# VectorE makes all weight remainders in both feed-forward products, with three edits at the borders between the stages

## The chip, the cores and the metric

One NeuronCore of a Trainium2 chip runs the whole program. The metric is the device time of one execution in microseconds (us). The kernel before was run three times: 2825.05, 2814.47 and 2814.90 us, median 2814.9 us.

## What is computed

Two layers of a decoder trunk, for 1024 prompt tokens and 32 sample tokens that share all weights. Layer 0 has a pooling and attention mixer, layer 1 a gated mixer; each is followed by a feed-forward block and a gated embedding. The change touches the feed-forward blocks only:

```python
D_MODEL = 1024; D_FF = 4 * D_MODEL
...
r = r + y                                   # after the mixer
h = rmsnorm(r, norm_ffn[i])
r = r + jnp.einsum('nlf,fd->nld', jnp.square(jax.nn.relu(jnp.einsum('nld,df->nlf', h, ffn_w1[i]))), ffn_w2[i])
h = rmsnorm(r, norm_ple[i])
gate = jax.nn.sigmoid(jnp.einsum('nld,de->nle', h, ple_w_gate[i]))
r = r + gate * jnp.einsum('nlp,pd->nld', p[i], ple_w_proj[i])
```

## The kernel before

**Tiles.** Activations lie with features on the 128 partitions and all 1056 tokens along the row. Every float32 operand is split in two: a rounded part that TensorE takes (`whi` for weights, `sh` for activations) and the remainder (`wlo`, `sl`). A product is the sum of three matmuls, whi·sh, whi·sl and wlo·sh. For weights, `w_split` (lines 147 to 165) has ScalarE copy the raw tile to `whi` (L153), and then another engine subtract it to give `wlo` (L157). That is GpSimd unless an engine is named; with `later=True` the subtraction is handed back as a function, for the caller to place. The subtraction also gives the raw tile's buffer back and starts the load of the next weights. `whi` and `wlo` have two buffers each, so the copy for the step after next starts when TensorE has finished the present step.

**Two products with seven multiplications.** `pair` runs the block of a layer ("0" and "1"; a third call, "m", does a mixer product and is left as it was). The first product makes the hidden activations in 8 chunks `c` of four tiles. Chunk 0 is plain (`gemm_phase`, evicted by `plain`); chunks 1 to 7 go through `product1`, seven multiplications `p` in the order 2, 4, 6, 1, 5, 3, 7, each on sums or differences of blocks. The second product runs `product2` for four `n`, seven `p` (order 4, 6, 2, 1, 5, 3, 7) and two halves `kt`. One multiplication of `product1` and one half of `product2` are both 48 matmuls of 264 columns. I call both a **unit**. `w_operand` makes the block sums of the weights on VectorE (L206, L210, L216, L217).

**What sets the order.** Engines' queues are written out by this program and worked off in the order written. `fill` is a clock that steps after every six matmuls, so eight steps make a unit; `fill.after(n, f)` writes f's instructions n steps later.

**Evictions.** In `product1`, `evac1` empties the PSUM bank of each of two `m`: ScalarE copies (L1301) for p = 4, 6, 2, VectorE adds (L1305) and scales (L1541) for the others. Multiplications that accumulate into a bank must wait for its eviction: 6 follows 4, and 5, 3, 7 follow 1. In `product2`, VectorE adds each of four banks to the residual tile `r` (L1494) after the second half, in the order m = 0, 3, 1, 2.

**Between the products.** `parts_of` takes a chunk's four hidden tiles, subtracts blocks (L1560, L1567; the functions t4 and minus) and stores the operands to DRAM, `hop` (L1551, L1561). The second product loads them back (`op_load`, L1409, into one `hx` and one `tmp` buffer) and splits them (`op_split`: ScalarE L1152, VectorE L1155). The pools `tmp` and `hx` have four buffers each; each chunk of `product1` takes two of either. `ahead2` does the first loads and splits while chunk 7 is multiplied. In the last `n`, `ple_piece` prepares the operands of the embedding block's product (ScalarE L257, L1603; VectorE L260; the sum of squares L1604 on GpSimd).

So a layer has three **borders**: (1) from the plain chunk 0 into chunk 1, (2) from the first product into the second, (3) from the second product into the embedding block (matmuls of L303).

## Time and profile before

| what | value |
|---|---|
| timed runs | 2814.47 to 2825.05 us, median 2814.9 |
| profiled execution | 2809.02 us, span of its instructions 2807.2 us |
| TensorE matmuls | 2663.4 us busy, 95% of the span |
| VectorE, ScalarE, GpSimd | 1753.1, 1119.9 and 1005.4 us busy |
| mean granted TensorE clock | 0.978 of full |

TensorE's busy share says that the sum of its pauses is small; where they are and what ended each is in the views quoted below. In those, PE is TensorE's matmuls, PEld its weight loads, DVE VectorE, ACT ScalarE, POOL GpSimd and SPq SyncE's DMA queue. Layer 0's feed-forward runs from 847 to 1489 us of the span, layer 1's from 2013 to 2659 us.

### The profile page before, as it was taken

The page shows a single profiled execution, that of the slowest core. Times are in us where ns is not written, and L with a number is a line of the kernel's source. Part 1 is how long each engine was busy: PE and PEld are TensorE (multiplying, and loading weights), DVE is VectorE, ACT ScalarE, POOL GpSimd, SP SyncE. Part 2 cuts the span into 40 slices and gives each one's busy share as a digit, 9 for nine tenths or more (in the row PEclk, how much of TensorE's full clock was granted, in tenths as well). Part 3 has the DMA queues.
Part 4 walks back from the last instruction along what each step waited for, and adds up shares of the span by engine and source line. Part 5 has one row for each costly group of instructions (what it writes and reads, how often), then busy time and mean ns, then how long its engine had stood idle before and what let it go on. Part 6 is the DMA issues. An engine that isn't in the chain of part 4 may idle for free. (4 is left out here: it accounts for less than half of the span.)

```text
span 2807.2 us, 48902 instructions
## 1 busy us (share of the span) xinstructions
PE 2663.4 (95%) x20190; PEld 2576.6 (92%) x20190; DVE 1753.1 (62%) x2370; ACT 1119.9 (40%) x1901; POOL 1005.4 (36%) x442
## 2 busy tenths in 40 slices
PE   8999999998988999999999999988899999999897
PEld 8998898987987999999999998988899999999896
DVE  7435435354375556788786455778745658887855
ACT  4343333334163333333344355234533343333543
POOL 3332233222253444222233343656344442222434
PEclk9999999999999999999999999999999999999998
DMA  5225334354634444744412223351344457343112
GB/s 170 73 86 134 97 113 138 104 143 153 221 127 156 145 145 146 276 170 154 146 55 78 89 80 96 73 168 47 133 124 157 146 180 281 133 141 127 51 64 102
DMA packets 159295, 366.53 MB, mean 131 GB/s; under 512 B 46528, under 2 KB 54752, under 8 KB 159072
## 3 DMA queue, kind: packets, MB, share of 16 engines
q1 hardware_dynamic: 158208, 362.59, 39.7%
q8 instruction: 159, 2.61, 0.4%
q10 hardware_dynamic: 864, 0.82, 0.1%
q14 instruction: 64, 0.52, 0.1%
HBM read 245.20 MB, written 105.15 MB: 125 GB/s over the span
## 5 line engine op out<-in xcount | busy, mean ns | idle before, releaser
L157 POOL TENSOR_TENSOR wlo<-wraw,whi 128x1024 fp32r<-128x1024 f32 x155 | 394.2, 2544 | 952.5 <-ACT whi L153 901.4
L157 POOL TENSOR_TENSOR wlo<-wr,whi 128x1024 fp32r<-128x1024 f32 x121 | 313.0, 2586 | 564.8 <-ACT whi L153 544.1
L1323 PE MATMUL PS<-sh,whi 128*128 128x264 f32 x2016 | 414.7, 287 | 36.0 <-ACT tmp L1301 21.3
L1479 PE MATMUL PS<-sh,whi 128*128 128x264 f32 x2016 | 408.0, 284 | 22.7 <-DVE r L1494 18.1
L1323 PE MATMUL PS<-sh,wlo 128*128 128x264 f32 x2016 | 414.6, 287 | 6.4 <-POOL wlo L157 6.2
L1323 PE MATMUL PS<-sl,whi 128*128 128x264 f32 x2016 | 414.2, 287 | 0.0
L1479 PE MATMUL PS<-sl,whi 128*128 128x264 f32 x2016 | 410.6, 286 | 1.2 <-DVE sl L1155 1.2
L1479 PE MATMUL PS<-sh,wlo 128*128 128x264 f32 x2016 | 410.4, 285 | 0.0
L1323 PEld LDWEIGHTS PS<-sh,whi 128*128 128x128 f32 x2016 | 318.8, 191 | 39.9 <-ACT tmp L1301 21.7
L153 ACT ACTIVATE whi<-wraw 128x1024 fp32r<-128x1024 f32 x181 | 191.5, 1058 | 370.8 <-DVE wraw L216 92.1
L1479 PEld LDWEIGHTS PS<-sh,whi 128*128 128x128 f32 x2016 | 314.1, 189 | 24.8 <-issue 20.2
L1323 PEld LDWEIGHTS PS<-sh,wlo 128*128 128x128 f32 x2016 | 316.3, 191 | 8.3 <-POOL wlo L157 8.3
L153 ACT ACTIVATE whi<-wr 128x1024 fp32r<-128x1024 f32 x153 | 162.3, 1061 | 394.5 <-PE PS L1479 267.5
L1323 PEld LDWEIGHTS PS<-sl,whi 128*128 128x128 f32 x2016 | 315.8, 190 | 0.0
L421 PE MATMUL g<-sh,whi 128*128 128x352 f32 x888 | 311.0, 350 | 4.1 <-DVE vsn L532 3.0
L1479 PEld LDWEIGHTS PS<-sl,whi 128*128 128x128 f32 x2016 | 312.9, 189 | 1.8 <-DVE sl L1155 1.8
L1479 PEld LDWEIGHTS PS<-sh,wlo 128*128 128x128 f32 x2016 | 313.8, 190 | 0.0
L423 PE MATMUL g<-sh,wlo 128*128 128x352 f32 x888 | 287.9, 324 | 0.0
L422 PE MATMUL g<-sl,whi 128*128 128x352 f32 x888 | 287.5, 324 | 0.0
L1494 DVE TENSOR_TENSOR r<-r,PS 128x528 f32<-128x528 f32 x252 | 168.2, 699 | 48.9 <-PE PS L1479 48.9
L421 PEld LDWEIGHTS g<-sh,whi 128*128 128x128 f32 x888 | 168.6, 190 | 25.9 <-issue 22.0
L1155 DVE TENSOR_TENSOR sl<-tmp,sh 128x528 fp32r<-128x528 f32 x124 | 168.0, 1388 | 25.4 <-ACT sh L1152 25.4
(340 smaller groups left out, 4697.6 us busy)
## 6 DMA issues: line engine op xcount, KB each, us to landing
hx<-hop SPq DMA_DIRECT2D x56, 528.0 KB, 4.6
tmp<-hop SPq DMA_DIRECT2D x56, 528.0 KB, 5.0
wr<-in_w SPq DMA_DIRECT2D x56, 512.0 KB, 4.3
hop<-tmp SPq DMA_DIRECT2D x108, 264.0 KB, 4.9
hop<-hx SPq DMA_DIRECT2D x84, 264.0 KB, 4.6
wr<-in_w1q SPq DMA_DIRECT2D x42, 512.0 KB, 4.1
wraw<-in_w_e SPq DMA_DIRECT2D x39, 512.0 KB, 3.3
rscr<-r SPq DMA_DIRECT2D x24, 528.0 KB, 3.0
```

The costliest lines, as they stand in the source:

```text
L153: ACT.activation(hi, raw, AF.Copy)
L157: (eng or POOL).tensor_tensor(lo, raw, hi.bitcast(F32), op=ALU.subtract)
L421: PE.matmul(ps[:, :CH], hi[:, ws], xh[:, cs], start=k == 0, stop=False)
L422: PE.matmul(ps[:, :CH], hi[:, ws], xl[:, cs], start=False, stop=False)
L423: PE.matmul(ps[:, :CH], lo[:, ws], xh[:, cs], start=False, stop=k == 7)
L1155: DVE.tensor_tensor(lo, x, hi.bitcast(F32), op=ALU.subtract)
L1323: PE.matmul(ps[:, n, :], a[:, ws], b[:, n * HT // 2:(n + 1) * HT // 2], start=first and k == 0 and i == 0, stop=k == 3 and i == 2, skip_gr ...
L1479: PE.matmul(ps[:, q, :], a[:, ws], b[:, q * HT // 2:(q + 1) * HT // 2], start=first and kt == 0 and k == 0 and i == 0, stop=kt == 1 and k ...
L1494: DVE.tensor_tensor(r, r, ps, op=ALU.add)
```

## The change

In layers 0 and 1: (a) `product1` no longer has GpSimd make the remainder; VectorE does, two steps behind the copy. (b) `product2` splits the weights at the third bank of both halves, the remainder on VectorE two steps later (before, one half did so, and the other had GpSimd make it). (c) The plain chunk's tiles 2 and 3 go to `hx` instead of `tmp`, and its block differences are written at steps 3, 6, 15, 22 like every other chunk's. (d) `ahead2` spreads eight operand splits over steps 34 to 48. (e) `ple_piece` adds its squares on VectorE.

```diff
@@ product1
-                    w_split(wptr[0] + 1)
+                    if l == "m":
+                        w_split(wptr[0] + 1)
+                    else:
+                        rest = w_split(wptr[0] + 1, DVE, True)
+                        if rest:
+                            fill.after(2, rest)
@@ ahead2
-                op_splits(0, k, 40 + k)
-                op_splits(2, k, 46 + k)
-            fill.after(47, lambda: op_load(1))
-            fill.after(53, lambda: op_load(3))
+                op_splits(0, k, 34 + 2 * k)
+                op_splits(2, k, 42 + 2 * k)
+            fill.after(46, lambda: op_load(1))
+            fill.after(54, lambda: op_load(3))
@@ product2
-                elif kt == 1 and i_m == 1 and not (last and p == 7):
-                    w_split(wptr[0] + 1)
-                elif kt == 0 and i_m == 2:
+                elif i_m == 2 and not (last and p == 7 and kt == 1):
                     rest = w_split(wptr[0] + 1, DVE, True)
                     if rest:
                         fill.after(2, rest)
@@ product2
-                    ple_piece(*pieces[p, kt, i_m], POOL, xp, gi)
+                    ple_piece(*pieces[p, kt, i_m], POOL if l == "m" else DVE, xp, gi)
@@ plain
-            u = h[0, j] = tmp()
+            u = h[0, j] = tmp() if j < 2 else h["pool"].tile([128, NT], F32, tag="hx", bufs=4, name=nm("hx"))
@@ begin
-            parts_of(c - 1, (1, 2, 4, 7) if c == 1 else (3, 6, 15, 22))
+            parts_of(c - 1, (3, 6, 15, 22))
```

VectorE's queue at border 1 of layer 0, from the first block difference of chunk 0 on. Before (`tmp_7745`, `tmp_7811`, `tmp_7920`, `tmp_8005` are the chunk's four tiles):

```order
L1567 TENSOR_TENSOR tmp_7745<-tmp_7745,tmp_7920 128x528
L1567 TENSOR_TENSOR tmp_7811<-tmp_7811,tmp_8005 128x528
L1567 TENSOR_TENSOR tmp_7745<-tmp_7745 128x528
L1567 TENSOR_TENSOR tmp_7811<-tmp_7811 128x528
L1567 TENSOR_TENSOR tmp_7920<-tmp_7920,tmp_7745 128x528
L1567 TENSOR_TENSOR tmp_8005<-tmp_8005,tmp_7811 128x528
L216 TENSOR_TENSOR wraw_7898<-wraw_7827,wr_7897 128x1024
L217 TENSOR_TENSOR wr_7894<-wr_7894,wr_7896 128x1024
```

The same place after the change (line 1567 has become 1570; `hx_7920` and `hx_8005` are tiles 2 and 3):

```order
L1570 TENSOR_TENSOR tmp_7745<-tmp_7745,hx_7920 128x528
L1570 TENSOR_TENSOR tmp_7811<-tmp_7811,hx_8005 128x528
L216 TENSOR_TENSOR wraw_7898<-wraw_7827,wr_7897 128x1024
L217 TENSOR_TENSOR wr_7894<-wr_7894,wr_7896 128x1024
L157 TENSOR_TENSOR wlo_8087<-wraw_7898,whi_8088 128x1024
L1570 TENSOR_TENSOR tmp_7745<-tmp_7745 128x528
L1570 TENSOR_TENSOR tmp_7811<-tmp_7811 128x528
L157 TENSOR_TENSOR wlo_8148<-wr_7896,whi_8149 128x1024
L1570 TENSOR_TENSOR hx_7920<-hx_7920,tmp_7745 128x528
```

The block sum of the weights, L216, now stands before the last four differences, and remainders (L157) stand between them.

VectorE's queue inside the second product of layer 0, one multiplication's four evictions and the next half. Before:

```order
L1494 TENSOR_TENSOR r_10963<-r_10963,PS 128x528
L1494 TENSOR_TENSOR r_10966<-r_10966,PS 128x528
L1494 TENSOR_TENSOR r_10964<-r_10964,PS 128x528
L1494 TENSOR_TENSOR r_10965<-r_10965,PS 128x528
L1155 TENSOR_TENSOR sl_97<-tmp_11278,sh_96 128x528 x2
L1155 TENSOR_TENSOR sl_83<-hx_11426,sh_82 128x528 x2
L157 TENSOR_TENSOR wlo_11614<-wr_8020,whi_11615 128x1024
```

The same place after the change (L1494 has become L1497):

```order
L1497 TENSOR_TENSOR r_10966<-r_10966,PS 128x528
L1497 TENSOR_TENSOR r_10969<-r_10969,PS 128x528
L1497 TENSOR_TENSOR r_10967<-r_10967,PS 128x528
L157 TENSOR_TENSOR wlo_11551<-wr_10979,whi_11552 128x1024
L1497 TENSOR_TENSOR r_10968<-r_10968,PS 128x528
L1155 TENSOR_TENSOR sl_97<-tmp_11278,sh_96 128x528 x2
L1155 TENSOR_TENSOR sl_83<-hx_11421,sh_82 128x528 x2
L157 TENSOR_TENSOR wlo_11614<-wr_8020,whi_11615 128x1024
```

A remainder has come in front of the fourth eviction.

VectorE's queue at border 3 of layer 0 (last `n`, where the second half of p = 3 is evicted), after the change (L1607 is the sum of squares that GpSimd made before):

```order
L157 TENSOR_TENSOR wlo_14306<-wr_10980,whi_14307 128x1024
L260 SCALAR_TENSOR_TENSOR sl_83<-r_10967,gains,sh_82 128x528
L1607 TENSOR_TENSOR acc<-acc,tmp_14332 128x528
L1497 TENSOR_TENSOR r_10970<-r_10970,PS 128x528
L260 SCALAR_TENSOR_TENSOR sl_85<-r_10968,gains,sh_84 128x528
L1607 TENSOR_TENSOR acc<-acc,tmp_14350 128x528
L1497 TENSOR_TENSOR r_10973<-r_10973,PS 128x528
L260 SCALAR_TENSOR_TENSOR sl_85<-r_10968,gains,sh_84 128x528
L1607 TENSOR_TENSOR acc<-acc,tmp_14368 128x528
L1497 TENSOR_TENSOR r_10971<-r_10971,PS 128x528
```

Before, the same rows stood there without the three L1607.

## Rows read from the trace of the kernel before

**Rows 1.** Who TensorE waited for, 820 to 1480: total, times, longest (us).

```profile
PE PS L1323 <- ACT tmp L1301: 10.7, 1, 10.7
PE PS L1479 <- DVE r L1494: 4.5, 1, 4.5
PE PS L1323 <- DVE tmp L1305: 3.1, 2, 2.5
```

**Rows 2.** Stretches inside the products: length, busy (count) per engine, clock, DMA share.

```profile
950.00:1000.00 50.00, 50.00 (x413) 50.00 (x412) 30.95 (x33) 19.68 (x26) 23.55 (x9) 1.00 0.43 149
1250.00:1300.00 50.00, 50.00 (x417) 50.00 (x417) 38.58 (x41) 18.87 (x28) 11.88 (x5) 1.00 0.49 161
```

**Rows 3.** The six borders in the same view, two rows a border, layer 0 first.

```profile
861.30:880.20 18.90, 8.13 (x52) 7.61 (x51) 5.10 (x6) 4.24 (x7) 4.73 (x2) 0.73 0.80 282
2026.40:2046.20 19.80, 9.07 (x50) 8.55 (x50) 5.10 (x6) 4.19 (x6) 4.73 (x2) 0.66 0.78 262
1142.90:1157.40 14.50, 9.53 (x64) 8.91 (x63) 13.55 (x16) 6.25 (x10) 3.12 (x2) 0.88 0.95 333
2309.90:2324.40 14.50, 9.72 (x64) 9.11 (x62) 13.61 (x16) 6.28 (x10) 3.13 (x2) 0.88 0.96 346
1468.50:1489.20 20.70, 13.75 (x98) 13.14 (x96) 18.91 (x17) 9.34 (x15) 14.95 (x8) 0.92 0.13 42
2636.90:2658.60 21.70, 14.79 (x98) 14.40 (x96) 18.79 (x17) 9.39 (x15) 14.82 (x8) 0.84 0.12 39
```

**Rows 4.** VectorE's groups by shape, 1200 to 1460: busy us, mean ns, idle before.

```profile
L1155 DVE TENSOR_TENSOR sl<-tmp,sh 128x528 fp32r<-128x528 f32 x45 | 67.1, 1527 | 12.0 <-ACT sh L1152 12.0
L1494 DVE TENSOR_TENSOR r<-r,PS 128x528 f32<-128x528 f32 x91 | 60.9, 699 | 18.9 <-PE PS L1479 18.9
L1155 DVE TENSOR_TENSOR sl<-hx,sh 128x528 fp32r<-128x528 f32 x44 | 28.9, 697 | 0.0
L157 DVE TENSOR_TENSOR wlo<-wraw,whi 128x1024 fp32r<-128x1024 f32 x9 | 11.0, 1223 | 3.2 <-ACT whi L153 2.9
```

**Rows 5.** VectorE in order of time at border 1: start, us, instruction, idle before.

```profile
858.97 1.32 DVE L1567 TENSOR_TENSOR tmp<-tmp,tmp 128x528 f32<-128x528 f32 x2
864.60 1.41 DVE L1567 TENSOR_TENSOR tmp<-tmp 128x528 f32<-128x528 f32 x2 [4.31 <-DMA hop<-tmp]
867.39 1.42 DVE L1567 TENSOR_TENSOR tmp<-tmp,tmp 128x528 f32<-128x528 f32 x2 [1.38 <-DMA hop<-tmp]
868.73 1.22 DVE L216 TENSOR_TENSOR wraw<-wraw,wr 128x1024 f32<-128x1024 f32 x1
```

**Rows 6.** ScalarE in order of time at border 1.

```profile
870.04 1.06 ACT L153 ACTIVATE whi<-wraw 128x1024 fp32r<-128x1024 f32 x1 [12.58 <-DVE wraw L216]
...
871.57 0.61 ACT L1301 ACTIVATE tmp<-PS 128x528 f32<-128x528 f32 x1
```

**Rows 7.** VectorE in order of time at border 2.

```profile
1138.92 3.56 DVE L1155 TENSOR_TENSOR sl<-hx,sh 128x528 fp32r<-128x528 f32 x2
...
1149.52 2.20 DVE L1541 SCALAR_TENSOR_TENSOR tmp<-tmp,rstd 128x528 f32<-128x528 f32 x1
```

**Rows 8.** DMA issues, 1115 to 1165: KB each, median us from issue to landing.

```profile
hx<-hop SPq DMA_DIRECT2D x4, 528.0 KB, 6.3
```

**Rows 9.** VectorE in order of time at border 3.

```profile
1458.59 2.51 DVE L1155 TENSOR_TENSOR sl<-tmp,sh 128x528 fp32r<-128x528 f32 x1 [0.20 <-ACT sh L1152]
...
1465.16 1.54 DVE L260 SCALAR_TENSOR_TENSOR sl<-r,gains,sh 128x528 fp32r<-128x528 f32 x1 [0.22 <-ACT sh L257]
1466.62 1.82 DVE L1155 TENSOR_TENSOR sl<-tmp,sh 128x528 fp32r<-128x528 f32 x1
1468.37 2.32 DVE L157 TENSOR_TENSOR wlo<-wr,whi 128x1024 fp32r<-128x1024 f32 x1
1470.62 1.80 DVE L260 SCALAR_TENSOR_TENSOR sl<-r,gains,sh 128x528 fp32r<-128x528 f32 x1
1472.34 0.69 DVE L1494 TENSOR_TENSOR r<-r,PS 128x528 f32<-128x528 f32 x1
```

## The prediction, made before the changed kernel ran

> **What bounds the kernel now.** I read the views in this order: the waits of TensorE, the busy time in stretches, VectorE's groups by shape, and the order of time at the borders.
>
> The waits view of layer 0's feed-forward holds three that matter: 10.7 us for ScalarE's eviction L1301, 4.5 for VectorE's eviction L1494, and 2.5 for VectorE's L1305 [rows 1]. Inside the products TensorE never pauses: 50.00 us busy of 50.00 at full clock, 413 matmuls in the first product (0.1211 us each) and 417 in the second (0.1199) [rows 2]. So what happens to a remainder there is worth nothing while it stays in time, and the change can gain only at the borders.
>
> What the borders cost is the length of each stretch less its matmuls at that pace [rows 3]. Border 1: 18.9 - 52 x 0.1211 = 12.6 us and, in layer 1, 19.8 - 6.1 = 13.7. Border 2: 14.5 - 64 x 0.1211 = 6.7 in both. Border 3: 20.7 - 98 x 0.1199 = 8.9 and 21.7 - 11.8 = 9.9. [...]
>
> **VectorE's durations hang on GpSimd.** The same subtraction of 528 columns takes 1527 ns in the mean from `tmp` and 697 from `hx` [rows 4]. A single one reads 0.70, or like 2.51 [rows 9] where a GpSimd remainder runs beside it. The addition that reads PSUM takes 699 ns in all 91 cases [rows 4]. Changes (a), (b) and (e) leave GpSimd idle in both products, so I price every VectorE subtraction at 0.70 from now on and a remainder at 1.22 [rows 4].
>
> **Inside the products.** First product: a unit is 48 x 0.1211 = 5.8 us. VectorE is busy 30.95 us of 50, that is 3.6 a unit [rows 2]; one remainder makes it 4.8, less the stretching. It fits. The new remainder stands after the eviction of the second bank and its scaling, which end 1.4 us into the next unit; the copy it waits for takes 1.06 [rows 6] and starts with the unit, so the remainder ends about 2.7 in. The next eviction falls due at 2.9. What was GpSimd's is needed at 5.8.
>
> Second product, one multiplication (two units, 11.6 us): four evictions, four splits and two remainders are 2.8 + 2.8 + 2.4 = 8.0 us; the block sums L206 to L217 are 8 of 1.22 in seven multiplications, 1.4 each. 9.4 of 11.6 fits, and it is no more than the 38.58 of 50 of now [rows 2] (9.0 of 11.6), because in those 260 us 45 x 0.83 = 37 us of stretching goes [rows 4], while one remainder of 1.22 comes in each of 22 multiplications, 27 us. The place to watch is the fourth eviction, now queued behind a remainder. That waits for its copy (1.06 into the next unit), ends at 2.3, and the eviction at 3.0. TensorE returns to that bank after three others, at 3 x 1.45 = 4.4. Slack 1.4 us: cost nothing, and if that cover is gone, see the second rival. Weights' loads and stored blocks that SyncE issues behind a remainder come about 1 us earlier, since VectorE ends sooner than GpSimd.
>
> **Border 1** (edit c, with the first two remainders). ScalarE's eviction stands behind a copy that waited 12.58 us for L216 [rows 6]. L216 stood behind four differences that overwrite tiles whose stores were still under way: VectorE idled 4.31 and 1.38 us for them [rows 5]. The new order puts L216 right after the two differences that wait for no store. They end at 858.97 + 1.32 = 860.3; L216 1.22, the copy 1.06 and the two evictions 0.59 + 0.61 (a row of either [rows 6] gives 0.6) end at 863.8 instead of 872.2. The buffers allow it: with tiles 2 and 3 in `hx`, chunk 1's first two `tmp` are free. So 2.3 us of the 10.7 stay. Behind such a wait border 2 shows clock 0.88 of 14.5 us [rows 3]; I charge 1.5 us for that. Border 1 then costs 3.8: a gain of 8.8 and 9.9, 18.7. Bounds: 0.5 us of cost if the rest hides too, all 26 us if the queue finds another reason to wait. I take the worked figure.
>
> **Border 2** (edit d). VectorE is the chain here: it is busy 13.55 of 14.5 us [rows 3]. GpSimd's stretching goes, 3.56 - 1.4 and 2.20 - 0.7 = 3.7 us [rows 7]. Two remainders come into the same stretch, 2.4. Splitting from step 34 instead of 40 moves two of 0.70 ahead into idle time, of which I count half. Gain 2.0 a layer, 4. Against it: `hx` loads take 6.3 us from issue to landing [rows 8], and the first split now stands 5 steps, 3.6 us, behind its load. If ScalarE waits 2.7 us there, and VectorE's evictions behind it, the gain is lost and up to 3 us more. Bounds -3 to +4 a layer.
>
> **Border 3** (edits b, e). Before the late eviction at 1472.34 five instructions were stretched: 2.51, 1.54, 1.82, 2.32 and 1.80 [rows 9] against 0.70, 0.76, 0.70, 1.22 and 0.76 unstretched, 5.9 us. Into the same piece come one remainder (1.22) and three sums of squares (0.70 each), 3.3. The eviction is 2.5 earlier, and 2.0 of the 4.5 us wait stays. Between the next evictions stand a split and a sum, so they follow at about 2.0 us where TensorE needs 1.45: three more waits of 0.5. The last evictions, which the embedding block's first matmul needs, were also stretched; some 0.5 us is left there of about 2.7. Border 3 then costs 4.0: a gain of 4.9 and 5.9, 10.8. Bounds: 0 (if the clock stays low over the small waits, and new sums eat the rest) and 17.
>
> **Sum.** 18.7 + 4.0 + 10.8 = 33.5 us. The profiled execution took 2809.0; 2775.5 is left. The median of the runs is 2814.9, 5.9 above it, so I forecast **2781 us** for the median.
>
> **A rule that speaks against the change.** Rows first: L216 did not overtake the differences that waited for stores [rows 5], so VectorE here works strictly in order, and a remainder that waits holds the eviction behind it. [...] By this rule the fourth eviction ends 3.0 us into the unit, without it 0.7: the sum is the same by both while 4.4 is the limit, but without it the second rival could not be, and by it that rival has its 6 in 100.
>
> **The rivals.**
>
> *Small gain (11 in 100).* The waits shrink, but TensorE keeps its low clock over the many short ones, and the early splits wait for their loads. Border 1 gains 14, border 2 nothing, border 3 about 5: 19 us, 2796. For it: every long wait in [rows 3] has a low clock behind it. Against: the inner stretches are at 1.00.
>
> *VectorE becomes the bound (6 in 100), slower.* If the long subtractions were not GpSimd's doing and 1527 ns stayed, a multiplication would need 9.4 + 2 x 0.83 = 11.1 us, and with about 1.8 us idle before each remainder that waits for its copy, some 12.6. It decides from 11.6 on; each multiplication then adds 1 us. There are 28 in a layer: 56 us more, less the 33.5 of the borders, 2837. Against: the PSUM additions at a steady 699 and the `hx` splits at 697 [rows 4].
>
> *No measurable gain (10 in 100).* Moving L216 up does not release border 1, because the copy's next condition (the weights, or the tile's other readers) comes as late; border 3's new sums replace what they remove. Gain about 4, 2811. Against: the rows at border 1 give each link.
>
> *More than worked (8 in 100).* The short waits hide too, and the clock stays up: 50 of the 58.5 us, 2765.
>
> **How the numbers follow.** The forecast (2770 to 2795) has 65 in 100, the rivals 35. A difference of 0.5%, 14 us, is about what a measurement of this kernel can tell from none. Faster by more: the forecast, the larger gain and most of the small one, 0.83; within: 0.11; slower: 0.06. The range from 2763 to 2802 leaves out the slow rival, most of the case without gain, and little below.
>
> **What would show it.** Right: GpSimd with almost no remainder between 850 and 1490; splits from `tmp` near 700 ns; the 10.7 us wait down to 2 to 3; L1494's 4.5 down to about 2; full busy shares inside the products; 0.121 us a matmul. Wrong: pauses of TensorE at L1479 inside the second product, waits for a remainder made by VectorE, or a wait at L1301 that stays at 10 us.

## The result and the profile after

The changed kernel takes 2771.6 us (median of four runs, 2767.8 to 2773.4), the kernel before 2815.2 us beside it: ratio 0.9835, 95% interval 0.9811 to 0.986 (it is taken over all runs, one of before at 2825 us among them; the two medians give 0.9845). By the medians it is 43.6 us faster; the forecast was 2781 us. The profiled execution took 2770.68 us (span 2768.9), 38.3 less than that of before.

First who TensorE waited for, in the same stretch of layer 0 as [rows 1] (L1484 is the old L1479, L1497 the old L1494, L1606 the old L1603):

```profile
PE PS L1323 <- DVE tmp L1305: 2.4, 1, 2.4
PE PS L1323 <- ACT tmp L1301: 2.0, 1, 2.0
PE PS L1484 <- DVE r L1497: 1.8, 2, 1.6
PE PS L303 <- ACT tmp L1606: 1.7, 1, 1.7
```

The 10.7 us for L1301 have become 2.0, and the 4.5 for L1494 1.8. The longest wait for L1305, 2.5, is still there as 2.4. The same view of before names two more (820 to 1490):

```profile
PE PS L303 <- ACT tmp L1603: 2.5, 1, 2.5
PE PS L1479 <- DVE tmp L1541: 1.8, 1, 1.8
```

The first has become 1.7; the second, for the scaling, is gone.

Then the busy time in stretches, as [rows 2] and [rows 3]: the two stretches inside the products, then borders 1, 2 and 3, layer 0 first.

```profile
950.00:1000.00 50.00, 50.00 (x413) 50.00 (x412) 32.88 (x39) 19.80 (x26) 0.00 (x0) 1.00 0.36 127
1250.00:1300.00 50.00, 50.00 (x417) 50.00 (x416) 35.49 (x46) 18.10 (x25) 0.00 (x0) 1.00 0.49 166
860.00:869.00 9.00, 6.95 (x57) 6.74 (x56) 6.42 (x8) 4.88 (x7) 0.00 (x0) 1.00 1.03 371
2008.30:2018.30 10.00, 7.95 (x53) 7.73 (x52) 6.50 (x8) 4.29 (x7) 0.00 (x0) 0.83 1.03 371
1134.00:1144.50 10.50, 8.08 (x52) 7.70 (x51) 10.31 (x12) 5.09 (x7) 0.00 (x0) 0.84 1.04 392
2283.80:2294.30 10.50, 8.14 (x53) 7.76 (x52) 10.36 (x12) 5.08 (x7) 0.00 (x0) 0.84 1.03 380
1453.80:1470.40 16.60, 13.00 (x99) 11.97 (x98) 15.83 (x24) 8.68 (x15) 0.00 (x0) 1.00 0.13 44
2603.60:2620.10 16.50, 13.02 (x100) 11.98 (x98) 15.79 (x24) 8.96 (x15) 0.00 (x0) 1.00 0.14 42
```

Inside the products nothing has changed: 413 and 417 matmuls in 50 us, as in [rows 2], while GpSimd does nothing (0.00). The borders, worked as in the prediction (length less matmuls at the inner pace), now cost 2.1 and 3.6, 4.2 and 4.1, 4.7 and 4.5 us. That is 23.2, where the six of before (12.6, 13.7, 6.7, 6.7, 8.9 and 9.9 in the prediction) make 58.5, a gain of 35.3.

A second account needs no pace: the length of each product, from the first matmul of L1323 to the first of the second product to the first of L303, read in the order of time.

| length, us | first product, layers 0 / 1 | second product, layers 0 / 1 | the four |
|---|---|---|---|
| before | 306.2 / 307.1 | 335.3 / 337.6 | 1286.3 |
| changed | 294.9 / 295.5 | 329.2 / 329.1 | 1248.7 |

By it the feed-forward blocks gained 37.6 us, nearly all of the 38.3 between the two profiled executions. Of this, 1.4 us can't be put down to the edits: layer 1's second product of before ran at a slightly slower pace, which other kernels show too (below, behind the table).

VectorE's groups between 1200 and 1460, as [rows 4]:

```profile
L1497 DVE TENSOR_TENSOR r<-r,PS 128x528 f32<-128x528 f32 x88 | 59.0, 698 | 4.7 <-PE PS L1484 4.7
L157 DVE TENSOR_TENSOR wlo<-wr,whi 128x1024 fp32r<-128x1024 f32 x30 | 36.7, 1225 | 40.6 <-ACT whi L153 40.6
L1155 DVE TENSOR_TENSOR sl<-tmp,sh 128x528 fp32r<-128x528 f32 x46 | 30.6, 702 | 0.0
L1155 DVE TENSOR_TENSOR sl<-hx,sh 128x528 fp32r<-128x528 f32 x44 | 29.1, 701 | 0.0
```

The subtraction from `tmp` has fallen from 1527 to 702 ns, the value that it had from `hx` in the same stretch; the addition that reads PSUM stays at 698. That `tmp` and `hx` differed before was a matter of time and not of the tile. In order of time, 20 of the 45 subtractions from `tmp` overlapped a GpSimd instruction and took 2.56 us in the mean, the other 25 took 0.70; none of the 44 from `hx` overlapped one. Four of the additions that read PSUM did, at 0.69 us each. Before each remainder that waits for its copy VectorE now stands idle, 40.6 us for 30 of them, 1.35 us each.

### The profile page after: what moved, and what is told of

It reads as the page before. It is cut to its first block, busy times and chain, and to the rows that moved or that the text cites. A ratio compares the mean times of both kernels' runs of the same rounds, so it can differ in the third digit from the quotient of the medians.

```text
span 2768.9 us, 48732 instructions
## 1 busy us (share of the span) xinstructions
PE 2650.0 (96%) x20190; PEld 2563.8 (93%) x20190; DVE 1780.0 (64%) x2542; ACT 1118.0 (40%) x1901; POOL 567.3 (20%) x270
## 5 line engine op out<-in xcount | busy, mean ns | idle before, releaser
L157 POOL TENSOR_TENSOR wlo<-wraw,whi 128x1024 fp32r<-128x1024 f32 x99 | 244.0, 2465 | 1875.3 <-ACT whi L153 1832.7
L1323 PE MATMUL PS<-sh,whi 128*128 128x264 f32 x2016 | 413.2, 286 | 17.3 <-DVE tmp L1305 4.8
L1323 PE MATMUL PS<-sh,wlo 128*128 128x264 f32 x2016 | 414.3, 287 | 5.9 <-POOL wlo L157 5.9
L1484 PE MATMUL PS<-sh,whi 128*128 128x264 f32 x2016 | 405.3, 283 | 14.2 <-DVE r L1497 12.8
L1323 PE MATMUL PS<-sl,whi 128*128 128x264 f32 x2016 | 413.9, 287 | 0.0
L1484 PE MATMUL PS<-sl,whi 128*128 128x264 f32 x2016 | 408.5, 284 | 1.2 <-DVE sl L1155 1.2
L1484 PE MATMUL PS<-sh,wlo 128*128 128x264 f32 x2016 | 409.4, 284 | 0.0
L1323 PEld LDWEIGHTS PS<-sh,whi 128*128 128x128 f32 x2016 | 318.1, 190 | 20.9 <-DVE tmp L1305 5.2
L1484 PEld LDWEIGHTS PS<-sh,whi 128*128 128x128 f32 x2016 | 313.8, 188 | 17.1 <-issue 11.0
L1323 PEld LDWEIGHTS PS<-sh,wlo 128*128 128x128 f32 x2016 | 316.4, 191 | 6.9 <-POOL wlo L157 6.9
L1323 PEld LDWEIGHTS PS<-sl,whi 128*128 128x128 f32 x2016 | 315.0, 190 | 0.0
L1484 PEld LDWEIGHTS PS<-sl,whi 128*128 128x128 f32 x2016 | 310.9, 188 | 1.8 <-DVE sl L1155 1.8
L1484 PEld LDWEIGHTS PS<-sh,wlo 128*128 128x128 f32 x2016 | 311.6, 189 | 0.0
L157 DVE TENSOR_TENSOR wlo<-wr,whi 128x1024 fp32r<-128x1024 f32 x128 | 156.6, 1223 | 180.1 <-ACT whi L153 180.1
L1497 DVE TENSOR_TENSOR r<-r,PS 128x528 f32<-128x528 f32 x252 | 168.9, 698 | 21.1 <-PE PS L1484 21.1
L422 PEld LDWEIGHTS g<-sl,whi 128*128 128x128 f32 x888 | 168.9, 190 | 1.4
```

What stands on the lines that cost most here:

```text
L157: (eng or POOL).tensor_tensor(lo, raw, hi.bitcast(F32), op=ALU.subtract)
L422: PE.matmul(ps[:, :CH], hi[:, ws], xl[:, cs], start=False, stop=False)
L1323: PE.matmul(ps[:, n, :], a[:, ws], b[:, n * HT // 2:(n + 1) * HT // 2], start=first and k == 0 and i == 0, stop=k == 3 and i == 2, skip_gr ...
L1484: PE.matmul(ps[:, q, :], a[:, ws], b[:, q * HT // 2:(q + 1) * HT // 2], start=first and kt == 0 and k == 0 and i == 0, stop=kt == 1 and k ...
L1497: DVE.tensor_tensor(r, r, ps, op=ALU.add)
```

## The experiments

Twelve kernels. Each table row gives the median of four runs, the ratio to the kernel before on the same chip, and the lengths of the products as above, in layers 0 / 1 of one profiled execution; "over" is the sum of the four less that of the changed kernel.

| kernel | median us | ratio (95%) | first product | second product | over |
|---|---|---|---|---|---|
| changed | 2771.6 | 0.9835 (0.9811 to 0.986) | 294.9 / 295.5 | 329.2 / 329.1 | 0 |
| undo_c | 2792.4 | 0.9926 (0.991 to 0.9943) | 305.0 / 303.6 | 329.2 / 330.6 | 19.7 |
| undo_a | 2785.6 | 0.9905 (0.989 to 0.992) | 301.9 / 301.0 | 330.9 / 330.9 | 16.0 |
| undo_b | 2777.4 | 0.9873 (0.9858 to 0.9889) | 294.9 / 294.0 | 330.7 / 333.4 | 4.3 |
| undo_d | 2772.7 | 0.9859 (0.9844 to 0.9874) | 293.2 / 293.8 | 332.0 / 330.3 | 0.5 |
| undo_e | 2781.8 | 0.9887 (0.9873 to 0.9902) | 293.4 / 294.0 | 334.9 / 335.1 | 8.7 |
| undo_ad | 2781.3 | 0.9886 (0.9871 to 0.9901) | 295.3 / 297.4 | 332.4 / 332.2 | 8.6 |
| gpsimd_inside | 2770.4 | 0.9848 (0.9834 to 0.9863) | 294.9 / 293.9 | 330.6 / 329.1 | -0.2 |
| second_bank | 2791.6 | 0.9919 (0.9902 to 0.9935) | 293.4 / 293.9 | 339.5 / 338.6 | 16.6 |
| evac_first | 2773.8 | 0.9869 (0.9851 to 0.9886) | 294.9 / 292.5 | 329.8 / 330.8 | -0.8 |
| late_pieces | 2772.9 | 0.9866 (0.9849 to 0.9884) | 293.4 / 294.0 | 330.2 / 327.4 | -3.8 |
| best | 2767.2 | 0.9846 (0.983 to 0.9861) | 292.8 / 291.1 | 330.4 / 330.4 | -4.0 |
| best2 | 2774.9 | 0.985 (0.9834 to 0.9867) | 297.6 / 296.5 | 327.4 / 329.0 | 1.8 |

Small differences in this table say little, for three reasons. First, the changed kernel was not timed again beside the others, and the kernel before had a median of 2815.2 us beside it, 2811.9 beside undo_a to undo_d, 2814.1 beside undo_e, undo_ad, gpsimd_inside and second_bank, 2811.6 beside evac_first, late_pieces and best, and 2815.5 beside best2. So up to 4 us of a difference of medians need not come from the edit. Second, apart from second_bank, TensorE goes through the inside of a second product at one of two paces, 0.1206 or 0.1211 us a matmul (417, or 415 to 416, in 50 us), with the clock at 1.00 in both. Before has one in each layer, the changed kernel the faster in both, undo_a and best the slower in both; undo_b, undo_e, undo_ad, gpsimd_inside and late_pieces have the slower in one layer. Over 2688 matmuls this makes 1.4 us in a length; what sets it is not shown. Third, stretches of low clock stand in other places from kernel to kernel (last section); in the changed kernel's products one costs some 1.7 us (0.83 or 0.84 of the 10 to 10.5 us above).

### undo_c: the order of the queue at border 1

```diff
-            u = h[0, j] = tmp() if j < 2 else h["pool"].tile([128, NT], F32, tag="hx", bufs=4, name=nm("hx"))
+            u = h[0, j] = tmp()
-            parts_of(c - 1, (3, 6, 15, 22))
+            parts_of(c - 1, (1, 2, 4, 7) if c == 1 else (3, 6, 15, 22))
```

> The changed kernel with edit (c) alone undone: the plain chunk's four tiles in tmp again, its differences at steps 1, 2, 4, 7. Theory (the order of VectorE's queue at border 1 is the whole of it): L216 stands behind the differences that wait for their stores again, the wait at L1301 is 10.5 to 11 us instead of 2.1, a low clock follows it, and both layers together lose the 21 us that border 1 gained: the first product's stage is 10 to 11 us longer in each layer, the rest of the program the same, about 2793 us in the median of runs. Rival (the remainders on VectorE did part of it): the loss is 15 us or less, because the copy that waits for L216 is followed by a remainder that no longer needs 2.5 us on GpSimd: about 2785 us.

Measured: 20.8 us in the medians, 19.7 in the products, nearly all in the first (10.1 and 8.0 us; 10 to 11 were expected). The wait is back (TensorE's waits, 820 to 1490):

```profile
PE PS L1323 <- ACT tmp L1301: 10.5, 1, 10.5
```

The theory holds: border 1's gain hangs on edit (c), and undoing (a) leaves this wait at 2.1 us. In the changed kernel VectorE and ScalarE do there what the prediction laid out (order of time, VectorE, then ScalarE):

```profile
857.66 1.32 DVE L1570 TENSOR_TENSOR tmp<-tmp,hx 128x528 f32<-128x528 f32 x2
858.90 1.22 DVE L216 TENSOR_TENSOR wraw<-wraw,wr 128x1024 f32<-128x1024 f32 x1
...
863.12 1.40 DVE L1570 TENSOR_TENSOR tmp<-tmp 128x528 f32<-128x528 f32 x2 [0.60 <-DMA hop<-tmp]
```

```profile
860.21 1.06 ACT L153 ACTIVATE whi<-wraw 128x1024 fp32r<-128x1024 f32 x1 [4.07 <-DVE wraw L216]
861.17 0.59 ACT L1301 ACTIVATE hx<-PS 128x528 f32<-128x528 f32 x1
861.66 0.60 ACT L1301 ACTIVATE tmp<-PS 128x528 f32<-128x528 f32 x1
```

L216 begins at 858.90, not 868.73 [rows 5], and the difference that waits for a store now stands behind it. The second eviction ends at 862.26, and TensorE, whose last matmul ends at 860.27, waits 2.0 us.

### undo_a, undo_d, undo_ad: border 2 and SyncE's queue

undo_a:

```diff
-                    if l == "m":
-                        w_split(wptr[0] + 1)
-                    else:
-                        rest = w_split(wptr[0] + 1, DVE, True)
-                        if rest:
-                            fill.after(2, rest)
+                    w_split(wptr[0] + 1)
```

> The changed kernel with edit (a) alone undone: GpSimd makes the first product's remainders again. Theory (inside the product nothing hangs on it): no pause of TensorE inside, border 1 as after the change (wait 2.1 us), border 2 worse because VectorE's two-tile subtractions beside GpSimd's remainders are stretched again from 0.70 to about 2 us: 1 to 4 us a layer, 2 to 8 us in all, 2774 to 2780 us. Rival 1 (the remainder on VectorE costs as much queue time at border 2 as the stretching did): no difference, 2772 us. Rival 2 (the remainder on GpSimd, 2.5 us instead of 1.22, is late at border 1): the first product's stage 3 us or more longer in each layer with a wait for POOL L157 at border 1.

undo_d:

```diff
-                op_splits(0, k, 34 + 2 * k)
-                op_splits(2, k, 42 + 2 * k)
-            fill.after(46, lambda: op_load(1))
-            fill.after(54, lambda: op_load(3))
+                op_splits(0, k, 40 + k)
+                op_splits(2, k, 46 + k)
+            fill.after(47, lambda: op_load(1))
+            fill.after(53, lambda: op_load(3))
```

> The changed kernel with edit (d) alone undone: the eight operand splits in one lump at steps 40 to 49. Theory (the splits in front of the last evictions and scalings were the second wait of border 2): the wait of about 2 us at the start of the second product, behind the scaling, comes back, the first wait of 2.5 us stays: 2 to 3 us a layer, 4 to 6 us in all, 2776 to 2778 us. Rival (the stretching by GpSimd was the cause, which edit (a) took away): no difference, 2772 us.

Neither came out as expected. Undoing (a) cost 14 us in the medians and 16.0 in the products, of which 2.8 are the slower pace in both second products; undoing (d) cost 0.5 in the products and 1.1 in the medians, no more than the noise. In undo_a the second rival shows in small, a wait of 0.7 us at border 1 for a remainder of GpSimd. The longest new wait is one of 1.8 us in chunk 7 (1.9 in layer 1), for an eviction `hx` of L1305. It begins on SyncE's queue (DMA issues in order of time, undo_a; L1409 loads an operand, L175 weights, L1549 stores):

```profile
1120.30 0.33 SPq L175 DMA_DIRECT2D wr<-in_w  x1
1120.72 0.86 SPq L1549 DMA_DIRECT2D hop<-tmp  x2
1121.67 0.41 SPq L1409 DMA_DIRECT2D hx<-hop  x1
1125.18 0.32 SPq L1409 DMA_DIRECT2D tmp<-hop  x1
```

```profile
1128.23 1.18 ACT L1152 ACTIVATE sh<-hx 128x528 fp32r<-128x528 f32 x2 [3.24 <-DMA hx<-hop]
```

The weights' load L175 stands behind the remainder, which GpSimd ends at 1120.27 (1117.85 and 2.42). Behind it in the queue stand two stores and the operand's load, which is issued at 1121.67 and lands some 6.5 us later; ScalarE waits 3.24 us, VectorE's split behind it, and the eviction behind that. The split takes 0.71 us, so the stretching that the theory named is not what makes this wait. In the changed kernel VectorE ends the same remainder sooner, in 1.23 us instead of 2.42, at 1116.00. There chunk 7's first addition L1305 begins at 1116.87, in undo_a at 1119.90, so the two clocks are 3.0 us apart; the load is earlier by more than that:

```profile
1116.02 0.33 SPq L175 DMA_DIRECT2D wr<-in_w  x1
1116.76 0.32 SPq L1414 DMA_DIRECT2D hx<-hop  x1
1117.17 0.38 SPq L1414 DMA_DIRECT2D tmp<-hop  x1
```

Against the matmuls that is 1.9 us earlier for `hx` (1121.67 - 3.0 - 1116.76) and 5.0 for `tmp`. So (d), which splits five steps behind the load, needs (a). If this is so, undoing both must cost less than (a) alone; that was the next run, both diffs together.

> Edits (a) and (d) both undone: GpSimd makes the first product's remainders and the eight operand splits come in one lump, with (b), (c) and (e) kept. Undoing (a) alone cost 14 us, undoing (d) alone 1. Theory (the early splits of (d) need the unstretched VectorE of (a); without (a) they hold evictions of chunk 7 back): undoing both costs less than undoing (a) alone, border 2 is back at 6.7 us a layer against 4.2 now: 5 to 8 us over the changed kernel, 2777 to 2780 us, and the wait of 2.0 us at L1305 in chunk 7 is gone. Rival (the remainder on GpSimd costs what it costs, whatever the order of the splits): 14 to 16 us over, 2786 us or more.

Measured: 8.6 us in the products (1.4 of it the slower pace), 9.7 in the medians, against 16.0 and 14.0 with (a) alone undone. The wait for `hx` in chunk 7 is gone, the one at the start of the second product is back (TensorE's waits, 820 to 1490):

```profile
PE PS L1479 <- DVE tmp L1539: 3.2, 1, 3.2
PE PS L1323 <- DVE tmp L1305: 3.1, 2, 2.5
```

The rival falls: the medians are 4.3 us apart, hardly beyond the noise, but the wait is gone in both layers. The two edits are not a sum: with (d) in, (a) is worth 16.0 us in the products; with (d) out, 8.1 (13.2 and 6.7 without the slower pace).

That undoing (d) alone hardly shows in the lengths does not make it worth nothing. Its wait at the start of the second product came back as expected (L1544, 2.7 us in layer 0, 1.2 in layer 1), so its rival, that (a) had taken the cause away, falls too, though it named the time. But in the profiled execution the clock in layer 0 was not low behind border 2's first wait: 1.00 from 1134 to 1144.5, 0.84 in the changed kernel. And TensorE came later to border 1, whose end VectorE and ScalarE set, and waited less there (0.6 instead of 2.0); that the low clock lay ahead of border 1 this time is an estimate from these two differences:

```profile
PE PS L1484 <- DVE tmp L1544: 2.7, 1, 2.7
...
PE PS L1323 <- ACT tmp L1301: 0.6, 1, 0.6
```

undo_e, second_bank and late_pieces, with (d) in and the same 1.00 behind border 2's first wait, wait 1.5 us for L1544 in layer 0 and not at all in layer 1. So (d) is worth about 1.2 us a layer, too little for the medians to show.

### undo_b and undo_e: border 3

```diff
-                elif i_m == 2 and not (last and p == 7 and kt == 1):
+                elif kt == 1 and i_m == 1 and not (last and p == 7):
+                    w_split(wptr[0] + 1)
+                elif kt == 0 and i_m == 2:
                     rest = w_split(wptr[0] + 1, DVE, True)
```

> The changed kernel with edit (b) alone undone: in the second product's other half GpSimd makes the remainder again. Theory (stretching is what border 3 had cost): subtractions from tmp are back at a mean near 1.5 us, TensorE stays at full pace inside the product, and before the late eviction at border 3 the stretched instructions put 2 to 4 us more on the wait (now 1.7 us): the second product's stage 3 to 6 us longer in each layer, 6 to 12 us in all, 2778 to 2784 us. Rival (the sums of squares on VectorE make the wait, whoever makes the remainder): under 2 us in all, 2772 us.

```diff
-                    ple_piece(*pieces[p, kt, i_m], POOL if l == "m" else DVE, xp, gi)
+                    ple_piece(*pieces[p, kt, i_m], POOL, xp, gi)
```

> The changed kernel with edit (e) alone undone: ple_piece's sums of squares on GpSimd again, all remainders on VectorE. Theory (each sum of squares takes 0.70 us of VectorE's queue in front of an eviction at border 3, but beside a GpSimd sum the splits L260 with two inputs stretch as they did): the two cancel, within 2 us a layer, 2768 to 2776 us. Rival (the new sums on VectorE are what is left of border 3's 1.7 us wait and the small ones behind it): the waits at L1484 shrink below 1 us and the second product is 1.5 to 3 us shorter in each layer, 2766 to 2769 us.

undo_b cost 5.8 us in the medians, a little under the theory's range, and 1.5 and 4.3 us in the second products; 1.4 of the 4.3 are the slower pace, and some 2 are low clock behind the waits (0.79 of full from 2603.6 to 2620.1, 1.00 in the changed kernel). The late eviction, where the theory put the loss, waits only 2.0 us for 1.6; a second wait, of 1.7 us in layer 0 and 0.9 in layer 1, stands behind it, where a split L260 takes 2.31 us instead of 0.76 beside a remainder of GpSimd. undo_e surprised both theories: 10.1 us in the medians, 5.7 and 6.1 us in the second products. The wait at L1484 did not shrink; it grew from 1.6 to 4.1 us. VectorE before that eviction, undo_e:

```profile
1455.89 1.83 DVE L1155 TENSOR_TENSOR sl<-tmp,sh 128x528 fp32r<-128x528 f32 x1
1457.64 2.33 DVE L157 TENSOR_TENSOR wlo<-wr,whi 128x1024 fp32r<-128x1024 f32 x1
1459.90 1.79 DVE L260 SCALAR_TENSOR_TENSOR sl<-r,gains,sh 128x528 fp32r<-128x528 f32 x1
1461.62 0.69 DVE L1497 TENSOR_TENSOR r<-r,PS 128x528 f32<-128x528 f32 x1
```

and GpSimd in the same time:

```profile
1452.72 1.38 POOL L1607 TENSOR_TENSOR acc<-acc,tmp 128x528 f32<-128x528 f32 x1 [8.18 <-ACT tmp L1606]
1455.36 7.49 POOL L1607 TENSOR_TENSOR acc<-acc,tmp 128x528 f32<-128x528 f32 x4 [1.26 <-ACT tmp L1606]
```

Four small sums on GpSimd stretch three of VectorE's instructions by 1.0 to 1.1 us each (1.83 against 0.70, 2.33 against 1.22, 1.79 against 0.76), 3.3 us together, more than four sums cost on VectorE (0.70 each). The sums suffer too, 1.87 us each in the row of four against 1.38 for the single one. The eviction, which reads PSUM and one tile, takes its 0.69 while GpSimd works. In the changed kernel the same place reads (VectorE):

```profile
1452.48 1.22 DVE L157 TENSOR_TENSOR wlo<-wr,whi 128x1024 fp32r<-128x1024 f32 x1
1453.62 0.76 DVE L260 SCALAR_TENSOR_TENSOR sl<-r,gains,sh 128x528 fp32r<-128x528 f32 x1
1454.30 0.70 DVE L1607 TENSOR_TENSOR acc<-acc,tmp 128x528 f32<-128x528 f32 x1
1454.91 0.70 DVE L1497 TENSOR_TENSOR r<-r,PS 128x528 f32<-128x528 f32 x1
```

By the second products alone (b) and (e) are worth 5.8 and 11.8 us (4.4 and 10.4 without the slower pace, low clock included), together more than the 9.6 that border 3 gained. The rows fit one reading: what counts is that GpSimd is silent there, and either edit undone breaks that. Both undone together was not run.

### gpsimd_inside: is anything gained inside?

```diff
-                    if l == "m":
+                    if l == "m" or 1 < c < n1 - 1:
                         w_split(wptr[0] + 1)
...
+                elif kt == 1 and 4 < 7 * n + ORDER.index(p) < 21:
+                    if i_m == 1:
+                        w_split(wptr[0] + 1)
                 elif i_m == 2 and not (last and p == 7 and kt == 1):
```

> GpSimd makes the remainders again, but only away from the borders: in chunks 2 to 6 of the first product, and in one half of each multiplication of the second product from the third multiplication of the first n to the end of the third n. At the borders (chunks 1 and 7, the last n) VectorE makes them as in the changed kernel. Theory (inside the products a remainder is worth nothing while it stays in time; the stretching there is hidden): VectorE's subtractions from tmp are long again inside, TensorE's pace inside stays at 0.121 us a matmul without a pause, 2769 to 2775 us. Rival (part of the 14 us of edit (a) and the 6 us of edit (b) was gained inside, by earlier loads of the weights or by less contention): 5 us or more over the changed kernel, 2777 us or more, with pauses of TensorE inside.

Measured: 2770.4 us, products 0.2 us shorter. Inside, GpSimd works again and the subtractions from `tmp` are long again (stretches, and VectorE's groups from 1200 to 1440):

```profile
950.00:1000.00 50.00, 50.00 (x413) 50.00 (x412) 26.69 (x31) 19.85 (x26) 23.34 (x9) 1.00 0.41 145
1250.00:1300.00 50.00, 50.00 (x415) 50.00 (x414) 39.19 (x44) 18.09 (x25) 10.41 (x4) 1.00 0.50 165
```

```profile
L1155 DVE TENSOR_TENSOR sl<-tmp,sh 128x528 fp32r<-128x528 f32 x42 | 52.4, 1284 | 7.3 <-ACT sh L1152 7.3
```

TensorE is at full busy share. The 415 matmuls instead of 417 in layer 0 are the slower pace, not a pause: layer 1 of the same kernel has 417 between 2400 and 2450. The theory holds: no gain of the remainders inside can be seen, it comes from the few at the borders (chunks 1 and 7, the ends of the second product).

### second_bank: how thick is the cover?

```diff
-                elif i_m == 2 and not (last and p == 7 and kt == 1):
+                elif i_m == 1 and not (last and p == 7 and kt == 1):
```

> The changed kernel with the second product's weights split at the second bank instead of the third, in both halves, so that VectorE's remainder stands in front of the third eviction instead of the fourth. In the trace of the changed kernel the fourth eviction ends 2.97 us into the next half, and TensorE comes back to that bank at 4.35. Theory (a queue in strict order, a remainder that cannot start before its copy): the third eviction now ends at about 2.97 and is needed at 2.90; every second half has a wait of 0.1 to 0.3 us at L1484 for L1497, 56 in the program: 6 to 17 us over the changed kernel, 2778 to 2789 us. Rival (some slack that I did not see, the copy may start earlier): no wait, 2772 us.

Measured: 20 us slower than the changed kernel in the medians. In the profile the second products are 10.3 and 9.5 us longer. Inside there are no waits that the waits view names, yet each stretch of 50 us holds 410 matmuls instead of 417:

```profile
1250.00:1300.00 50.00, 50.00 (x410) 49.49 (x409) 34.48 (x46) 19.62 (x29) 0.00 (x0) 1.00 0.50 173
```

That is 0.122 us a matmul for 0.1199, 0.2 us in each multiplication of 96, the size that the theory gave, and some 5 to 6 us a layer. VectorE (order of time) shows the queue:

```profile
1279.94 1.23 DVE L157 TENSOR_TENSOR wlo<-wr,whi 128x1024 fp32r<-128x1024 f32 x1 [1.04 <-ACT whi L153]
1281.09 0.69 DVE L1497 TENSOR_TENSOR r<-r,PS 128x528 f32<-128x528 f32 x1
```

The rest of the products' loss is mostly at border 3, where the wait at L1484 is 3.5 us (1.6 in the changed kernel), the one at L303 2.8 (1.7), and the clock is 0.90 of full from 1453.8 to 1470.4 (1.00). So the cover in the changed kernel, one bank's time, is real and no thicker than 1.4 us. Another 7.5 us of that profile lie in the mixer's product, which the edit does not touch; it was the slowest of the four runs (2797.5), and this part is left unexplained.

### evac_first, late_pieces, best, best2: can the rest go?

evac_first:

```diff
                 if m == 1:
+                    if l != "m":
+                        evac1(c, p, m, ps)
...
-                evac1(c, p, m, ps)
+                if l == "m" or m == 0:
+                    evac1(c, p, m, ps)
```

> The changed kernel with one more move in the first product: the second bank's eviction is issued before the block sums and the copy of the next weights (L206, L210, L153), not behind them. Theory (of border 2's first wait, 2.5 us, all is the eviction L1305 standing behind two block sums of 1.22 us and two operand splits): the eviction runs as soon as the bank is done, the wait goes to under 0.3 us, and the low clock behind it (1.7 us) goes as well or moves: 5 to 8 us less in both layers together, 2764 to 2767 us. Border 1 stays at 2.1 us, since the copy that waits for L216 still stands in front of the next eviction. Rival (a wait takes its place): the operand splits or the scaling are late at the start of the second product by as much, 2770 to 2773 us.

late_pieces (in both layers; `M_AT` is `PLE_AT` without features 5 and 6, whose second halves `M_LATE` takes up later):

```diff
-    xs, fs = pair(0, xs, "left", "right", [], 2, ffn_parts, slots0, PLE_AT, eo_lead)
+    xs, fs = pair(0, xs, "left", "right", [], 2, ffn_parts, slots0, M_AT, eo_lead)
-    ple(0, ..., ple0_next, ple_lead, ple0_last, (0, 3, 1, 2, 4, 5, 6, 7))
+    ple(0, ..., ple0_next, lambda k: ple_lead(k, M_LATE), ple0_last, (0, 3, 1, 2, 4, 5, 6, 7))
```

> The changed kernel with two pieces (features 5 and 6, second half) taken from before the second product's last four evictions to behind them, into the first columns of the embedding block's product, as the mixer layer already has it. Theory (VectorE's queue before the last evictions is what the wait of 1.8 and 1.7 us at L303 is): 2.9 us less stands before them, the wait goes to under 0.3 us, and with what low clock follows it 3 to 6 us are gained in both layers together, 2766 to 2769 us; the wait of 1.7 us at L1484 before stays. Rival (the pieces are late where the embedding block needs features 5 and 6): a wait at L303 for L260 of 1 us or more, 2771 to 2775 us.

best, both of these and:

```diff
-            parts_of(c - 1, (3, 6, 15, 22))
+            parts_of(c - 1, (9, 13, 19, 26) if c == 1 else (3, 6, 15, 22))
```

> Both of the last two moves, and the plain chunk's differences at steps 9, 13, 19 and 26 instead of 3, 6, 15 and 22, so that the block sum L216 at border 1 stands in front of the first two of them as well (2.6 us of VectorE). Theory (every border wait that is left is an order in a queue): border 1's 2.1 us go to under 0.5, 3 to 4 us in both layers, on top of what the two moves give alone: 2755 to 2763 us. Rival (the limit is another one there, the copy L153 or the landing of the weights): border 1 stays at 1.5 us or more, 2762 to 2768 us.

evac_first gained nothing (2773.8). The eviction no longer stands behind the block sums, but a remainder that waits for its copy now stands before it, and the wait is 1.8 us for 2.4: the rival, with another instruction in the lead. late_pieces shortened the wait at L303 to 0.6 us for 1.7 (under 0.3 was expected), gained 3.8 us in the products and nothing that the medians can tell (2772.9). best takes border 1's wait away: none at L1301 is left, and layer 1 has one of 0.5 us for a remainder in its place. It has the lowest median, 2767.2 us, and products 4.0 us shorter, but stays above the 2755 to 2763 expected. The kernel before ran at 2811.6 us beside it, so its ratio, 0.9846, is no better than the changed kernel's 0.9835: no gain over that kernel is shown. The limit at border 2 in best (VectorE, order of time):

```profile
1132.26 1.22 DVE L157 TENSOR_TENSOR wlo<-wr,whi 128x1024 fp32r<-128x1024 f32 x1 [1.04 <-ACT whi L153]
1133.41 0.70 DVE L1155 TENSOR_TENSOR sl<-hx,sh 128x528 fp32r<-128x528 f32 x1
1134.02 0.70 DVE L1305 TENSOR_TENSOR tmp<-tmp,PS 128x528 f32<-128x528 f32 x1
```

best2 moves that remainder behind the eviction:

```diff
-                            fill.after(2, rest)
+                            fill.after(5, rest)
...
             elif k == 7:
-                w_split(wptr[0] + 1)
+                w_split(wptr[0] + 1, None if l == "m" else DVE)
```

> The last kernel with two moves more: the first product's remainder five steps behind its copy instead of two, that is behind the first bank's eviction instead of in front of it; and the remainder of the first product's first weights on VectorE, which stands idle there, instead of GpSimd. Theory (at border 2 the remainder that waits about 1 us for its copy holds the eviction L1305, as the fourth eviction is held inside the second product): the wait of 1.8 us at L1305 and the one of 1.1 us for L157 go under 0.5 us each, and the wait of 1.7 us at the start of the first product is 1.1 us shorter; 4 to 7 us in both layers together, 2760 to 2763 us. Rival (the remainder also gives back the raw weights' buffer, so the next weights' load goes out 2.2 us later and the block sums that read them are late): waits for DMA or for L206 inside the first product, 2767 us or more.

In this kernel one remainder of each layer, that of the second half (`kt` = 1) of the second product's first multiplication, is taken after the next block sum has overwritten its raw tile, so that operand's low part is another number; instructions and shapes are the same. Measured: 2774.9 us for 2760 to 2763 expected. The eviction's wait is down to 0.6 us, and the remainder is now late itself (TensorE's waits, 820 to 1490; the longest is at border 1):

```profile
PE PS L1323 <- DVE wlo L157: 4.1, 3, 2.3
...
PE PS L1323 <- DVE tmp L1305: 0.6, 1, 0.6
```

Neither theory had that wait. VectorE is busy 10.31 of 10.5 us at border 2 in the changed kernel: there an instruction moved ahead of one wait makes another.

## Why the prediction was right

**Inside the products, zero: right.** gpsimd_inside shows no gain there, and second_bank that the cover of the fourth eviction is as thin as worked. In the changed kernel TensorE's half ends at 1280.3, where the copy starts; the remainder begins at 1281.43 and the eviction behind it ends at 1283.27, 2.97 us in (worked: 3.0):

```profile
1281.43 1.23 DVE L157 TENSOR_TENSOR wlo<-wr,whi 128x1024 fp32r<-128x1024 f32 x1 [1.59 <-ACT whi L153]
1282.57 0.70 DVE L1497 TENSOR_TENSOR r<-r,PS 128x528 f32<-128x528 f32 x1
```

**Border 1, 18.7: measured 20.6.** The wait left over was to be 2.3 us and is 2.0 and 2.1. The term that was off is the 1.5 us of low clock in each layer: in layer 0 the clock stayed at 1.00 through the wait, in layer 1 it was 0.83 of 10 us, 1.7 us.

**Border 2, 4.0: measured 5.1.** The first wait stays and the second is gone; the term named neither. It took (a) and (d) for a sum, and gave no price to weights' loads and stores that come "about 1 us earlier". undo_a shows that operand loads 1.9 and 5.0 us earlier are the condition for (d): without them the case of the lower bound (ScalarE waits for the landing, evictions behind it) is what happens, with 3.24 us.

**Border 3, 10.8: measured 9.6.** The eviction's wait was to be 2.0 and is 1.6 us; the small waits behind it are two of 0.1 to 0.2 us instead of three of 0.5. The wait at L303 was to be 0.5 us and is 1.7 and 1.5: pieces, each with a split and a new sum, stand before the last four evictions. late_pieces moves two of them away and leaves 0.6; undo_e, with the sums on GpSimd, has 2.5, so the sums alone are not the cause.

**The sum, 33.5: 35.3 by the borders, 37.6 by the lengths.** The 2.3 us between lie in what the border windows do not hold: 1.4 are the slower pace in layer 1's second product of before, and 0.7 a wait for a GpSimd remainder in layer 1's first product, which is gone. The errors of the three terms, 1.9 and 1.1 us too little and 1.2 too much, partly cancel, which is luck. The 9.4 us between 2781 and 2771.6 are 4.8 of the profiled execution (2775.5 forecast, 2770.7 taken) and 4.6 of the step from it to the median: 5.9 us before, 0.9 now. The prediction carried that step over from one set of runs to the next, and no term of it covers the change.

**The rivals.** VectorE did not become the bound: its stretching went, since it came only where a GpSimd instruction ran beside it (2.56 us for 0.70 before, from 1200 to 1460; 702 ns in the mean now). (That rival's own sum slips: 11.1 and 1.8 make 12.9, not 12.6; the idle time before a remainder, for which the prediction names no row, is 1.35 us.) The small gain and no gain fell with border 1. "More than worked" fell by its mechanism, for 23.2 us of border are left where it had 8.5; its 2765 us are nearer to the measured median than the forecast is.

## What to carry to other kernels

When two engines can make the same operand, find out which instructions slow each other, and price the move only where a wait is open: the same move showed no gain inside the products and was worth some 14 us in the medians at the first product's borders (edit (a), with (d) in place). Follow also what the slow instruction holds back: the buffer that it releases, the load behind that in the same queue, and the instruction that this load feeds. Edits that share a queue need not be a sum, so undo them one by one and in pairs.

## What had not been expected of the hardware

- GpSimd and VectorE slow each other: in undo_e four sums of 528 columns on GpSimd took 1.87 us each instead of 1.38, and put 1.0 to 1.1 us on each of three VectorE instructions. Moving four sums of 0.70 us off VectorE cost it more than they take there, 3.3 us against 2.8.
- The clock fell behind one wait and not behind an equal one: 2.05 us at border 1 in layer 0 and 2.06 in layer 1, granted clock 1.00 (860 to 869) and 0.83 (2008.3 to 2018.3). Nor did it fall at one border in every kernel: from 1134 to 1144.5, at border 2 in layer 0, it was 0.84 in the changed kernel, which costs 1.7 us, and 1.00 in undo_d, undo_e, second_bank and late_pieces, where the wait at border 1 before it was 0.6 to 0.7 us instead of 2.0. An estimate from these two: in the four kernels the low clock lay ahead of border 1, and since ScalarE's eviction ends the wait there, it only made the wait shorter, by 1.3 to 1.4 us. So such a stretch moves between stages from kernel to kernel; differences of 1.7 us in one stage say nothing.
